# Stores of the expert gates moved from GpSimd's DMA queue to SyncE's, one at a time between weight loads

## The chip, the cores and the metric

The kernel runs on one core of a Trainium2 chip. The metric is the device time of one execution in microseconds. Before the change the median of three runs is 3434.36 us (3432.82 to 3434.39). The profile that is quoted below comes from one further execution, which took 3430.97 us; its span, from the first to the last instruction, is 3429.2 us. A difference of 0.2% is 6.9 us.

## The reference, cut to what matters

The model is one layer: an attention mixer, and then a mixture of 16384 experts (PEER), of which each token takes 16 for each of 8 heads. Only the second half matters here:

```
q = (xb @ w_q).reshape(PEER_BLOCK, PEER_HEADS, 2, PEER_HALF)
s = jnp.einsum('thcd,hcnd->thcn', q, sub_keys).astype(jnp.float32)
s1, i1 = lax.top_k(s[:, :, 0], PEER_TOPK)
s2, i2 = lax.top_k(s[:, :, 1], PEER_TOPK)
...
g = jax.nn.softmax(top_s, axis=-1).reshape(PEER_BLOCK, -1)
idx = idx.reshape(PEER_BLOCK, -1)
h = jnp.einsum('tkd,td->tk', u[idx], xb)
act = (g * jax.nn.gelu(h.astype(jnp.float32), approximate=False)).astype(xb.dtype)
return jnp.einsum('tk,tkd->td', act, v[idx])
```

Here `u` and `v` have 16384 rows of 2048 numbers each, and there are 512 tokens.

## The kernel before, in words

**Two ways to the experts.** The kernel treats 336 of the 512 tokens densely: it multiplies them with the whole of `u` and later with the whole of `v`, and sets to zero what the routing did not choose. The other 176 tokens go the sparse way: the chosen rows of `u` and `v` are gathered, 128 rows of 8 KB (1 MB) by one indirect DMA, and VectorE multiplies each such tile with the tokens (line 1619, 2.28 us each).

**The activations stage.** The change lies in the stage that multiplies with `u`, about 1450 to 2405 us of the profile. It runs over 128 pieces `e` of the key, each in two halves, so 256 halves. A half (`u_half`, line 1349) loads one weight block `wr` of 512 KB from `ut` by SyncE's DMA queue (line 264). ScalarE rounds it to `wh` (line 265), VectorE subtracts and leaves `wl` (line 266), and TensorE makes 8 times 3 products of 128x128 weights with 336 columns (lines 277 to 279). There are four buffers `wr` and about four pairs `wh` and `wl`, so the loads run some four halves ahead. After each pair of halves ScalarE takes the gelu into `hb` and sends it to DRAM, to `h_d` (168 KB, ScalarE's own DMA queue).

**Rows beside it.** The gathers (`row`, line 1605) are issued by GpSimd on its own DMA queue. Four row buffers are in turn, so GpSimd can issue a gather only when VectorE is done with an older row. Where a row product stands among VectorE's instructions is fixed when the program is built, and so VectorE waits in place for a row that has not landed, with the `wl` behind it.

**Gates beside it.** For the dense tokens the softmax weights must be spread over all 16384 experts. `gates_of` does this four tokens at a time in one PSUM bank (line 1504). `gate_out` copies banks with ScalarE into two buffers `gb`, one for each half of the experts (line 1528). Eight banks make a block of 32 tokens. When the last bank of a block is copied, four DMAs store the block to `g_d` in DRAM, two from each buffer (line 1535): 512 KB each, from 4 KB in a row per partition to runs of 512 B in DRAM (two 16-token groups of 4 experts, 4 bytes). Eleven blocks make 44 stores; the third block is half as large. The two buffers belong to the next block as soon as their stores have landed, so the first copy of the next block waits for them. `hold=3` says how many filled banks must be there before the first bank of a block is copied. The next stage reads `g_d` and `h_d`.

**What sets the order.** The program is written in one order and then scheduled: within an engine instructions keep a fixed order from then on, and an instruction waits in place. DMAs of SyncE go through hardware queue q1, those of ScalarE through q10, those of GpSimd through software queue q0. The 16 DMA engines serve all three.

Of the kernel before, what the change touches and what calls it, by code (L numbers as in the profile page):

```python
# [20 lines left out]
NOSYNC = mybir.DependencyInfo(mybir.DependencyClass.NoSync, mybir.DependencyReason.DATA)  # L21
# [30 lines left out]
SB = 16  # L52
# [3 lines left out]
NG = NK // GRP  # L56
# [178 lines left out]
def body(tc, nc, a, dbg=None):  # L235
    V, S, T, G, SP = nc.vector, nc.scalar, nc.tensor, nc.gpsimd, nc.sync
# [6 lines left out]
    def ps_tile(name="ps"):  # L243
        return pp.tile([P, 512], F32, name=name, tag="ps")

    more = {"n": 0, "pool": None, "of": (4, (1,)), "raw": None, "raws": 0}
# [8 lines left out]
    def wtile(src, eng=None, parts=False):  # L255
        more["n"] += 1
        extra = more["pool"] is not None and more["n"] % more["of"][0] in more["of"][1]
        w_ = more["pool"] if extra else wp
        raw = raw_half()
        hi = w_.tile([P, 1024], F32R, name="wh", tag="wh")  # L260
        lo = w_.tile([P, 1024], F32R, name="wl", tag="wl")

        def load(s):
            SP.dma_start(raw[:, s], src[:, s])
            more["last"] = S.activation(hi[:, s], raw[:, s], AF.Copy)  # L265
            more["lo"] = (eng or V).tensor_sub(lo[:, s], raw[:, s], hi[:, s].bitcast(F32))  # L266

        if parts:
            return hi, lo, load
        load(slice(0, 1024))  # L270
        return hi, lo

    def front(name, m=0, hf=0, eng=None, parts=False):
        return wtile(a["front"][FIDX[(name, m, hf)]], eng, parts)

    def mm3(ps, wh, wl, xh, xl, start, stop):
        T.matmul(ps, wl, xh, start=start, stop=False)  # L277
        T.matmul(ps, wh, xl, start=False, stop=False)  # L278
        T.matmul(ps, wh, xh, start=False, stop=stop)  # L279

    def split(hi, lo, src, eng=None):
        S.activation(hi, src, AF.Copy)
        (eng or V).tensor_sub(lo, src, hi.bitcast(F32))
# [30 lines left out]
    g_d = dp.tile([NG, P, ND // SB, GRP, SB], F32, name="g_d")  # L314
# [25 lines left out]
    xh = xq.tile([P, KC, XW], F32R, name="xh")[:, :, :LEN]  # L340
# [657 lines left out]
    def branch_tile(i):  # L998

        raw = raw_half()  # L1000
        SP.dma_start(raw, a["front"][FIDX[(*branch[i], 0)]])
        hi, lo = (wp.tile([P, D], F16, name=x, tag=x)[:, :1024] for x in ("wh", "wl"))
        scaled(hi, lo, raw, b_sc[:, i:i + 1])
        return hi, lo
# [133 lines left out]
    for m in range(KC):  # L1138
# [6 lines left out]
        wh, wl = branch_tile(m)  # L1145
        ps = ps_tile()
# [33 lines left out]
    with tc.tile_pool(name="outp", bufs=2, side="right") as op:  # L1180
# [13 lines left out]
        for m in range(KC):  # L1194
# [4 lines left out]
            wh, wl = wparts.pop(m)  # L1199
# [5 lines left out]
            ps = ps_tile()  # L1205
# [69 lines left out]
    def spread_rows():  # L1275
        b0 = ND - (NT - 1) * P
        SP.dma_start(eob_d, er[b0:])
        SP.dma_start(gwb_d, gw_all[b0:, NT - 1])
        for j, nt in enumerate(PARTS):
            t = slice(AT[j], AT[j + 1])  # L1280
            for to, of in ((eob, eob_d), (gwb, gwb_d)):
                SP.dma_start(to[:, t], of[t].rearrange("t (r k) -> (t r) k", k=nt))
# [65 lines left out]
    def u_half(ps, e, hf):  # L1348
        wh, wl = wtile(a["ut"][2 * e + hf])
        for kc in range(8):  # L1350
            s = slice(kc * P, (kc + 1) * P)
            kk = hf * 8 + kc
            mm3(ps[:, :ND], wh[:, s], wl[:, s], hgh[:, kk, :ND], hgl[:, kk, :ND], kk == 0, kk == KC - 1)

    early = route(3, 2, rk)
    with tc.tile_pool(name="score", bufs=2, side="left") as sp_, \
# [34 lines left out]
        for hc in range(16):  # L1391
            ps = ps_tile()
            for hf in range(2):
                wh, wl = wq.pop((hc, hf)) if (hc, hf) in wq else front("wq", hc, hf, G if hf and hc != 1 else V)
# [76 lines left out]
    def after_gelu(ins):  # L1471
        if "gelu" in more:
            tc.add_manual_dep(ins.ins, more["gelu"].ins.name, NOSYNC, reason="not before its block")
# [39 lines left out]
    banks = []  # L1513
    gs = {"sent": 0, "done": 0, "pool": None, "gated": False, "six": None}

    def gate_out(hold=3):

        for _ in range(min(2, len(banks))):
            if banks[0][1] % TB == 0 and len(banks) < hold:
                return  # L1520
            ps, tok, w = banks.pop(0)
            b, o = tok // TB, tok % TB
            wb = min(TB, ND - b * TB)
            if o == 0:
                gb["now"] = [vi.tile([P, D], F32, name="gb", tag="gin")[:, :NK // 2 * wb]
                             .rearrange("p (g b j t) -> p g b j t", b=wb // SB, j=GRP, t=SB) for _ in range(2)]
            for hf, half in enumerate(gb["now"]):
                after_gelu(S.activation(half[:, :, o // SB, :, o % SB:o % SB + w],
                                        ps.rearrange("p (t f g j) -> p f g j t", t=4, f=2, j=GRP)[:, hf, :, :, :w],
                                        AF.Copy, scale=1.0 / GW))  # L1530
                if o + w == wb:
                    for q in range(2):
                        g0 = hf * NG // 2 + q * NG // 4
                        b0 = b * TB // SB
                        G.dma_start(g_d[g0:g0 + NG // 4, :, b0:b0 + wb // SB].rearrange("g p b j t -> p g (b j t)"),
                                    half[:, q * NG // 4:(q + 1) * NG // 4].rearrange("p g b j t -> p g (b j t)"))

    routed = []

    def routing():  # L1540
        for ti in (2, 0, 1):
            yield from route(ti, 4, rk)
            routed.append(ti)
            while routed:
                yield

    def gating():
        for _ in range(NT):
            while not routed:
                yield  # L1550
            g_ = gates_of(routed[0])
            next(g_)
            routed.pop()
            yield
            yield from g_
        while banks:
            gate_out(1)
            yield
        gs["gated"] = True
# [3 lines left out]
    steps, gate_steps = routing(), gating()  # L1563
# [86 lines left out]
    def group_in(g):  # L1650

        if g in (0, 3):
            lent.clear()
        if not 0 < g < 3:
            lent["h"] = hin_tile()
            lent["g"] = vi.tile([P, D], F32, name="gin", tag="gin")[:, :GRP * ND].rearrange("p (b j t) -> p b j t", j=GRP, t=SB)
        held[g] = [lent["h"], lent["g"]]
        in_order(SP.dma_start(lent["h"], h_d[g]))
        in_order(SP.dma_start(lent["g"], g_d[g]))

    def gated(h, g):

        q = h.rearrange("p j (b t) -> p b j t", t=SB)
        in_order(V.tensor_mul(q, q, g))

    def rows_due(pos):
        while gs["done"] < np.interp(pos, PACE[0], PACE[1]):
            n = gs["done"]
            row_step(more["lo"], 6 if gs["six"] is not None and gs["six"] + 1 <= n < OWN - 6 else 4 if n < OWN - 4 else 3)
# [3 lines left out]
    for e in range(NK):  # L1673
        g = e // GRP
        if e == NK // 2:
            spread_rows()
        if e == NK - 4:
            assert next(steps, steps) is steps and next(gate_steps, steps) is steps
            assert gs["done"] >= OWN
            group_in(0)  # L1680
        ps = ps_tile() if e else ps0
        for hf in range(2):
            if (e, hf) != (0, 0):
                u_half(ps, e, hf)
            next(gate_steps, None)
            if (e, hf) == (NK - 1, 0):
                gated(*held[0])
                parts = {0: [vi.tile([P, D], F32R, name=x, tag=t)[:, :GRP * VW].rearrange("p (j t) -> p j t", t=VW)[:, :, :ND]
                             for x, t in (("vah", "gin"), ("val", "hin"))]}
                split(*parts[0], held.pop(0)[0])  # L1690
                group_in(1)
            if hf == 0:
                rows_due(e)
            for _ in range(1 if e < 20 or e % 2 else hf):
                next(steps, None)
        hb = up.tile([P, ND], F32, name="hb")
        more["gelu"] = S.activation(hb, ps[:, :ND], AF.Gelu)
        S.dma_start(h_d[g][:, e % GRP], hb)
        rows_due(e + 0.5)
# [102 lines left out]
    for i, step in enumerate(STEPS):  # L1802
        if i == NG - 1:
            assert gs["done"] == len(todo)
            ln_exp(more["last"])
            for j, y in enumerate((gw_all.rearrange("p a b -> p (a b)"), columns(2))):
                t = slice(ND + AT[j], ND + AT[j + 1])
                V.tensor_add(acc[:, :, t], acc[:, :, t], y.rearrange("p (c t) -> p c t", c=KC))
            for c in range(0, KC, 4):
                ps = ps_tile()  # L1810
# [7 lines left out]
        for qi, (g, q8) in enumerate(step):  # L1818
            wh, wl = wtile(a["vb"][at])
# [14 lines left out]
            for dc in range(2):  # L1834
# [7 lines left out]
                ps = banks_of.pop(c) if goes_on else ps_tile()  # L1842
# [44 lines left out]
```

## Time and profile before

| what | value |
|---|---|
| median of the runs | 3434.36 us |
| the profiled execution, its own time | 3430.97 us |
| its span | 3429.2 us |
| TensorE busy | 3393.8 us (99% of the span) |
| VectorE busy | 2627.0 us (77%) |
| ScalarE busy | 1707.2 us (50%) |
| mean rate of all DMAs | 272 GB/s |
| stores of full blocks of gates | 40, 512 KB each, 14.0 us from issue to landing (median) |
| weight loads of the stage | 256, 512 KB each, 8.6 us (median) |

In the profile a busy share is a mean over stages. TensorE is busy almost all the time, so what matters is where it waits, and what it then waits for. Lines are written as L277 for line 277. `PEclk` or the clock in a window is the share of full speed that TensorE was granted. A DMA queue's share is the time that its packets took, as a part of the time of 16 engines.

### The profile page before, as it was taken

Reading aid. Unit: us, or ns where it says so; the run is one execution under the profiler, and the core shown is the slowest. Engines: PE = TensorE matmul, PEld = TensorE weight load, DVE = VectorE, ACT = ScalarE, POOL = GpSimd, SP = SyncE. Lnnn points to the kernel's source line nnn. Section 1 sums busy time; section 2 is a strip of 40 time slices with the busy share of each in tenths; the row PEclk is TensorE's granted clock in tenths of the full one; section 3 lists DMA queues with packets and bytes.
Section 4 is the critical chain, followed back from the end, with each engine's and each line's share of the span. In section 5 each row is a group of like instructions: output and inputs, shape, how many; then the busy total and the mean of one; then the engine's idle time right before and its main releaser. Section 6 shows DMA issues by size and latency. Waiting matters only on the chain.

```text
span 3429.2 us, 54600 instructions
## 1 busy us (share of the span) xinstructions
PE 3393.8 (99%) x21188; PEld 2891.4 (84%) x21188; DVE 2627.0 (77%) x3829; ACT 1707.2 (50%) x2901; POOL 711.2 (21%) x526
## 2 busy tenths in 40 slices
PE   9999999999999999999999999999999999999998
PEld 8766666657764458899999999999999999999998
DVE  7744444446556668999989788887889899999996
ACT  6665665555465543334756666663433333333335
POOL 0000000000002221112222233334322222233330
PEclk9999999999999999999999999999999999999999
DMA  6443443333256442379999999999999999999993
GB/s 235 136 145 131 140 133 111 133 111 105 80 180 214 154 137 91 102 278 355 353 382 348 381 415 414 411 416 414 385 373 377 385 389 385 393 401 396 402 386 113
DMA packets 236372, 933.39 MB, mean 272 GB/s; under 512 B 27120, under 2 KB 52688, under 8 KB 190928
## 3 DMA queue, kind: packets, MB, share of 16 engines
q1 hardware_dynamic: 142672, 487.40, 39.2%
q0 software_dynamic: 58160, 396.32, 29.0%
q10 hardware_dynamic: 35280, 46.18, 3.8%
q8 instruction: 166, 2.72, 0.3%
q14 instruction: 94, 0.77, 0.1%
HBM read 861.59 MB, written 68.21 MB: 271 GB/s over the span
## 4 chain that ended last, share of the span: by engine, by line
PE 81%; DVE 5%; issue 5%; DMA 5%; POOL 2%; ACT 1%; SPq 0%; POOLq 0%; DVEq 0%; ACTq 0%
PE ps L277 26%; PE ps L278 25%; PE ps L279 25%; DMA row<-u,eo 2%; POOL row L1605 1%; DVE wl L266 1%; DMA wr<-ut 1%; DMA row<-u,eob 1%; PE ps L1504 1%; DVE xgb L1623 1%; DVE row L1619 1%; DMA wr<-vb 0%; DMA hin<-h_d 0%; ACT wh L265 0%; PE ps L965 0%
## 5 line engine op out<-in xcount | busy, mean ns | idle before, releaser
L265 ACT ACTIVATE wh<-wr 128x1024 fp32r<-128x1024 f32 (+1 forms) x578 | 604.6, 1053 | 914.3 <-PE ps L279 648.3
L266 DVE TENSOR_TENSOR wl<-wr,wh 128x1024 fp32r<-128x1024 f32 (+1 forms) x565 | 680.7, 1215 | 150.2 <-ACT wh L265 147.9
L277 PE MATMUL ps<-hgh,wl 128*128 128x336 f32 (+1 forms) x2304 | 755.3, 328 | 10.0 <-DVE wl L266 10.0
L278 PE MATMUL ps<-hgl,wh 128*128 128x336 f32 (+1 forms) x2304 | 746.6, 324 | 0.0
L279 PE MATMUL ps<-hgh,wh 128*128 128x336 f32 (+1 forms) x2304 | 745.9, 324 | 0.0
L277 PE MATMUL ps<-vah,wl 128*128 128x336 f32 x2048 | 645.6, 315 | 2.4 <-DVE wl L266 2.4
L279 PE MATMUL ps<-vah,wh 128*128 128x336 f32 x2048 | 645.2, 315 | 0.0
L278 PE MATMUL ps<-val,wh 128*128 128x336 f32 x2048 | 645.2, 315 | 0.0
L277 PEld LDWEIGHTS ps<-hgh,wl 128*128 128x128 f32 x2304 | 433.1, 188 | 21.9 <-DVE wl L266 12.3
L279 PEld LDWEIGHTS ps<-hgh,wh 128*128 128x128 f32 x2304 | 433.1, 188 | 10.3 <-issue 0.2
L278 PEld LDWEIGHTS ps<-hgl,wh 128*128 128x128 f32 x2304 | 433.5, 188 | 9.6 <-issue 0.2
L277 PE MATMUL ps<-xnh,wl 128*128 128x512 f16 (+1 forms) x1184 | 392.7, 332 | 0.0
L279 PE MATMUL ps<-xnh,wh 128*128 128x512 f16 (+1 forms) x1184 | 392.6, 332 | 0.0
L278 PE MATMUL ps<-xnl,wh 128*128 128x512 f16 (+1 forms) x1184 | 392.6, 332 | 0.0
L277 PEld LDWEIGHTS ps<-vah,wl 128*128 128x128 f32 x2048 | 384.4, 188 | 2.7 <-DVE wl L266 2.7
L278 PEld LDWEIGHTS ps<-val,wh 128*128 128x128 f32 x2048 | 384.4, 188 | 0.0
L279 PEld LDWEIGHTS ps<-vah,wh 128*128 128x128 f32 x2048 | 384.4, 188 | 0.0
L1619 DVE SCALAR_TENSOR_TENSOR row<-row,xg 128x2048 f32<-128x2048 f32 x128 | 292.3, 2284 | 20.9 <-DMA row<-u,eo 20.8
L279 PEld LDWEIGHTS <-wh 128*128 128x128 f16 x1696 | 165.9, 98 | 143.9
L277 PEld LDWEIGHTS <-wl 128*128 128x128 f16 x1696 | 168.8, 100 | 135.2 <-issue 1.8
L278 PEld LDWEIGHTS <-wh 128*128 128x128 f16 x1696 | 165.9, 98 | 131.8 <-issue 0.3
L1605 POOL DMA_INDIRECT row<-u,eo x128 | 164.8, 1287 | 520.8 <-DVE row L1619 441.4
(608 smaller groups left out, 5378.9 us busy)
## 6 DMA issues: line engine op xcount, KB each, us to landing
wr<-ut SPq DMA_DIRECT2D x256, 512.0 KB, 8.6
wr<-vb SPq DMA_DIRECT2D x256, 512.0 KB, 7.8
wr<-front SPq DMA_DIRECT2D x164, 512.0 KB, 4.0
xr<-front SPq DMA_DIRECT2D x58, 512.0 KB, 4.6
h_d<-hb ACTq DMA_DIRECT2D x128, 168.0 KB, 8.1
gin<-g_d SPq DMA_DIRECT2D x32, 672.0 KB, 11.5
hin<-h_d SPq DMA_DIRECT2D x32, 672.0 KB, 8.9
g_d<-gb POOLq DMA_DIRECT2D x40, 512.0 KB, 14.0
```

The source lines that it names most:

```text
L265: more["last"] = S.activation(hi[:, s], raw[:, s], AF.Copy)
L266: more["lo"] = (eng or V).tensor_sub(lo[:, s], raw[:, s], hi[:, s].bitcast(F32))
L277: T.matmul(ps, wl, xh, start=start, stop=False)
L278: T.matmul(ps, wh, xl, start=False, stop=False)
L279: T.matmul(ps, wh, xh, start=False, stop=stop)
L1504: T.matmul(bank[:, o:o + P], ohs[q % 4][:, 1, :, t], wos[:, q % 3, c, :, t], start=c == 1, stop=c == 0)
L1605: G.indirect_dma_start(out=row, out_offset=None, in_=a[src], in_offset=bass.IndirectOffsetOnAxis(ap=idx, axis=0))
L1619: ins = V.scalar_tensor_tensor(row, row, 1.0, x, ALU.mult, ALU.mult, accum_out=wk)
L1623: ins = V.scalar_tensor_tensor(x, row, wk, x, ALU.mult, ALU.add)
```

## The change

Three things are changed. The stores of a block are no longer issued by GpSimd when the block is full: they are put in a list, `to_store`. In each half of the stage, after its products, one of them is taken from the list and issued by SyncE, in the queue of the weight loads; a dependency without a wait keeps it from being scheduled ahead of that half's last product. And `hold` goes from 3 to 4, so that the first copy of a block is written when four banks are there.

```diff
@@ def mm3
-        T.matmul(ps, wh, xh, start=False, stop=stop)
+        more["pe"] = T.matmul(ps, wh, xh, start=False, stop=stop)
@@
-    def gate_out(hold=3):
+    def gate_out(hold=4):
...
-                        G.dma_start(g_d[g0:g0 + NG // 4, :, b0:b0 + wb // SB].rearrange("g p b j t -> p g (b j t)"),
-                                    half[:, q * NG // 4:(q + 1) * NG // 4].rearrange("p g b j t -> p g (b j t)"))
+                        to_store.append((g_d[g0:g0 + NG // 4, :, b0:b0 + wb // SB].rearrange("g p b j t -> p g (b j t)"),
+                                         half[:, q * NG // 4:(q + 1) * NG // 4].rearrange("p g b j t -> p g (b j t)")))
+
+    to_store = []
+
+    def store_gates():
+
+        if to_store:
+            ins = SP.dma_start(*to_store.pop(0))
+            tc.add_manual_dep(ins.ins, more["pe"].ins.name, NOSYNC, reason="not before its place")
...
             if (e, hf) != (0, 0):
                 u_half(ps, e, hf)
+            store_gates()
             next(gate_steps, None)
```

TensorE's instructions keep their order. On SyncE the four stores of a block now stand between weight loads. This is SyncE after the change, at the eighth block (its buffers are gb_20848 and gb_20849):

```order
L264 DMA wr_21546<-ut 128x1024
L1543 DMA g_d_78<-gb_20848 128x8x128
L264 DMA wr_21591<-ut 128x1024
L1543 DMA g_d_78<-gb_20848 128x8x128
L264 DMA wr_21642<-ut 128x1024
L1543 DMA g_d_78<-gb_20849 128x8x128
L264 DMA wr_21686<-ut 128x1024
L1543 DMA g_d_78<-gb_20849 128x8x128
L264 DMA wr_21733<-ut 128x1024
```

Before, nothing but weight loads stood here, and the four stores stood on GpSimd, between two gathers. This is GpSimd before, where the ninth block's stores stand (gb_21487 and gb_21488):

```order
L1605 DMA row_22045<-u,eob_11479 128x2048
L1605 DMA row_22093<-u,eob_11479 128x2048
L1535 DMA g_d_78<-gb_21487 128x8x128 x2
L1535 DMA g_d_78<-gb_21488 128x8x128 x2
L1605 DMA row_22134<-u,eob_11479 128x2048
L1605 DMA row_22182<-u,eob_11479 128x2048
```

After the change these gathers follow each other without a store between them. The third place is ScalarE, where the ninth block's first bank is copied. Before (gb_21487 and gb_21488 are the ninth block's buffers, and wh the rounded weights):

```order
L265 ACTIVATE wh_21458<-wr_21457 128x1024
L1698 DMA h_d_77<-hb_21314 128x336
L265 ACTIVATE wh_21506<-wr_21505 128x1024
L1510 ACTIVATE wos_13513<-rh__10118,wt_13515 128x128 x4
L1510 ACTIVATE wos_13513<-more_oh_13512,wt_13515 128x128 x4
L1697 ACTIVATE hb_21403<-ps_21320 128x336
L1528 ACTIVATE gb_21487<-ps_21265 128x16x4x4
L1698 DMA h_d_77<-hb_21403 128x336
L1528 ACTIVATE gb_21488<-ps_21265 128x16x4x4
```

The same place after the change (the ninth block's buffers are now gb_21576 and gb_21577):

```order
L265 ACTIVATE wh_21547<-wr_21546 128x1024
L1707 DMA h_d_77<-hb_21403 128x336
L265 ACTIVATE wh_21592<-wr_21591 128x1024
L1510 ACTIVATE wos_13513<-rh__10118,wt_13515 128x128 x4
L1510 ACTIVATE wos_13513<-more_oh_13512,wt_13515 128x128 x4
L1706 ACTIVATE hb_21492<-ps_21409 128x336
L1528 ACTIVATE gb_21576<-ps_21262 128x16x4x4
L1707 DMA h_d_77<-hb_21492 128x336
L1528 ACTIVATE gb_21577<-ps_21262 128x16x4x4
L265 ACTIVATE wh_21643<-wr_21642 128x1024
L265 ACTIVATE wh_21687<-wr_21686 128x1024
```

The first copy of the block now stands two roundings of weights later. In SyncE's rows above, the last store of gb_20849, for which the copy into gb_21577 waits, stands behind the load of wr_21686. Its rounding, and that of wr_21642, come on ScalarE only after this copy.

More of the change, by code (lines that the diff above doesn't have):

```diff
@@ L1677, in body @@
         if e == NK - 4:
-            assert next(steps, steps) is steps and next(gate_steps, steps) is steps
+            assert next(steps, steps) is steps and next(gate_steps, steps) is steps and not to_store
             assert gs["done"] >= OWN
```

## Prediction

> **What bounds the kernel now.** I read the page first: TensorE is busy almost all the time.
>
> ```profile
> span 3429.2 us, 54600 instructions
> ...
> PE 3393.8 (99%) x21188; PEld 2891.4 (84%) x21188; DVE 2627.0 (77%) x3829; ACT 1707.2 (50%) x2901; POOL 711.2 (21%) x526
> ```
>
> So a change that leaves TensorE's work alone can win only what TensorE waits, 35.4 us in the whole span, or add to it. Where in the activations stage does it wait? The windows (instructions' busy time in each stretch, then clock, DMA share and GB/s) tell it by place.
>
> ```profile
> 1860.00:1940.00 80.00, 80.00 (x573) 78.72 (x573) 69.06 (x77) 53.21 (x130) 27.86 (x23) 1.00 0.97 367
> 1940.00:2340.00 400.00, 398.38 (x2804) 392.46 (x2803) 340.34 (x371) 256.29 (x614) 136.17 (x111) 1.00 1.02 414
> 2340.00:2360.00 20.00, 16.71 (x103) 16.44 (x102) 11.24 (x9) 6.07 (x7) 8.69 (x5) 0.95 1.02 411
> 2360.00:2380.00 20.00, 20.00 (x128) 20.00 (x128) 18.17 (x18) 5.49 (x7) 15.94 (x7) 0.97 1.02 417
> ```
>
> Two things are to be seen. From 1940 us on the DMA engines are full (share 1.02, 414 GB/s), and before that they are not. And TensorE loses 1.62 us in 400 us, then 3.29 us in one place, after which its clock is granted at 0.95 and 0.97. TensorE's own waits, for 2040 to 2365 us and for 2365 to 2420 us:
>
> ```profile
> PE ps L277 <- DVE wl L266: 4.9, 3, 3.3
> ...
> PE ps L277 <- DVE wl L266: 2.7, 2, 1.5
> ```
>
> The longest of the first three is followed back in the timeline of GpSimd and VectorE.
>
> ```profile
> 2328.20 0.94 POOL L1605 DMA_INDIRECT row<-u,eob  x1 [4.85 <-DVE row L1619]
> 2329.13 3.65 POOL L1535 DMA_DIRECT2D g_d<-gb  x4
> 2333.08 1.41 POOL L1605 DMA_INDIRECT row<-u,eob  x1 [0.30 <-issue]
> ...
> 2343.38 1.22 DVE L266 TENSOR_TENSOR wl<-wr,wh 128x1024 fp32r<-128x1024 f32 x1
> 2353.33 2.29 DVE L1619 SCALAR_TENSOR_TENSOR row<-row,xgb 128x2048 f32<-128x2048 f32 x1 [8.73 <-DMA row<-u,eob]
> 2355.55 2.35 DVE L266 TENSOR_TENSOR wl<-wr,wh 128x1024 fp32r<-128x1024 f32 x2
> ```
>
> Four stores of gates stand in GpSimd's queue ahead of a gather. The gather, issued at 2333.1, lands at 2353; VectorE waits 8.73 us for it, and two `wl` are stuck behind. TensorE waits 3.3 of these 8.73 us, so it had about 5.4 us of weights in hand. That is the lead on which the rest turns. All waits of this kind, of 1940 to 2365 us:
>
> ```profile
> ACT wh L265 <- DMA wr<-ut: 71.9, 39, 2.9
> ...
> DVE row L1619 <- DMA row<-u,eo: 20.0, 4, 7.7
> ...
> DVE row L1619 <- DMA row<-u,eob: 14.9, 3, 8.7
> ACT gb L1528 <- DMA g_d<-gb: 12.0, 4, 5.1
> ```
>
> VectorE waits 34.9 us for rows in seven waits, ScalarE 12.0 us in four for stores. ScalarE waits 39 times for a weight load: most loads land just when they are needed.
>
> **The change part by part.** First what goes.
>
> ```profile
> L1535 POOL DMA_DIRECT2D g_d<-gb x44: 887/928/992, 1673.0 to 2331.9; - x44
> ...
> L264 SPq DMA_DIRECT2D wr<-ut x256: 327/328/403, 1416.9 to 2430.8; - x128
> ```
>
> GpSimd loses 44 issues of 0.93 us, SyncE gains 44 of some 0.33 us, as for its loads; neither is near its limit, and this is worth nothing by itself. The gathers no longer stand behind the stores, so I take off the row waits' part of TensorE's time: 4.9 us, and the clock's loss after the longest, 0.05 x 20 + 0.03 x 20 = 1.6 us. That is 6.5 us. The 2.7 us after 2365 us lie behind the last store and stay; what if they went too is a bound below.
>
> Then what comes. The stores are the same bytes, in the queue of the weights. The queues in the full stretch, 1940 to 2340 us (packets, MB, share of 16 engines; below, issues and median us to landing):
>
> ```profile
> q0 software_dynamic: 15871, 103.93, 63.0%
> q1 hardware_dynamic: 14444, 52.62, 32.7%
> q10 hardware_dynamic: 7200, 8.60, 5.9%
> ...
> wr<-ut SPq DMA_DIRECT2D x100, 512.0 KB, 10.0
> g_d<-gb POOLq DMA_DIRECT2D x24, 512.0 KB, 14.6
> ...
> row<-u,eo POOLq DMA_INDIRECT x48, 11.3
> ```
>
> There are six bursts of four stores here, 12.6 MB. Weights take q1 at 131 GB/s (100 loads of 0.524 MB in 400 us, one in 4 us). And between bursts, 2098 to 2134 us:
>
> ```profile
> q0 software_dynamic: 1252, 9.11, 60.7%
> q1 hardware_dynamic: 1366, 5.01, 34.2%
> ...
> wr<-ut SPq DMA_DIRECT2D x10, 512.0 KB, 12.7
> ```
>
> With rows queued, q1 gets 5.01 MB in 36 us, 139 GB/s: hardly more than the weights need. A store ahead of a load in q1 then costs that load 0.524 MB / 139 GB/s = 3.8 us, four cost 15.1 us. This is the upper bound: 15.1 - 5.4 of lead = 9.7 us of waiting per burst. Lower bound: with no rows queued q1 gets all 414 GB/s, four stores take 5.1 us, the lead covers them, and TensorE waits 0. Which of the two? With the stores gone from it q0 needs 91.3 of the 165.6 MB that 414 GB/s move in 400 us, q10 8.6; 65.7 MB are left for q1, which now wants 65.2. So the engines are full to the last, and q1 gets 164 GB/s on the mean. Four stores at that rate take 12.8 us; in the four halves over which they go out, 16 us, the 33 GB/s that weights leave carry 0.53 MB, 3.2 us; 9.6 us of lateness against 5.4 us of lead leave 4.2 us. While VectorE waits for weights it frees no row buffers, gathers stop, and q1 gets their share, 63%; so I take somewhat over half of the 4.2 us, 2.4 us per burst. Six bursts are 14.4 us. Before 1940 us I take nothing: the DMAs are not full there, and the lead covers the stores.
>
> ScalarE is the second place. In the order printed above, the copy into the ninth block's second buffer waits for a store that stands behind two weight loads, both of which ScalarE rounds only after this copy. Queued behind it are those two `wh`, then their `wl`, then TensorE. Where the next copy comes two halves later than before, it moves by some 8 us, and the store's landing moves by its place behind two more loads and three stores. Today's longest such wait is 5.1 us. I keep it inside the 2.4 us, as the store and the loads share one queue, but it pushes towards the upper bound. The one bank more that stays filled costs TensorE nothing as long as the eight PSUM banks come round: none of TensorE's waits above is for ScalarE. If that cover went, the price would be one such copy's wait, up to 5.1 us per burst.
>
> The sum against the profiled execution: 3430.97 - 6.5 + 14.4 = 3438.9 us. The median of the runs is 3.4 us above that execution, so the forecast is 3442.3 us, 7.9 us slower.
>
> **The rivals.** *Heavy: the hardware queue moves the stores in short packets.* A store's runs in DRAM are 512 B. How queues cut runs is seen from 1268 to 1287 us, where GpSimd loads runs of 1344 B (xn) and ScalarE stores 64 KB in rows of 512 B (xc_d), and in the burst at 2145 to 2150 us (last row, q0 with stores):
>
> ```profile
> q0 software_dynamic: 768, 2.75, 46.2%
> ...
> q10 hardware_dynamic: 144, 0.07, 1.9%
> ...
> xn<-ht_d POOLq DMA_DIRECT2D x15, 168.0 KB, 4.1
> xc_d<-sc ACTq DMA_DIRECT2D x1, 64.0 KB
> ```
>
> ```profile
> q0 software_dynamic: 326, 1.21, 63.1%
> ```
>
> q0 has 3.6 KB per packet where the runs are 1344 B, and 3.7 KB with the stores: it joins runs. q10 has one packet per run. Its 64 KB took 1.9% of 19 us on 16 engines, 5.8 us; eight times that is 46 us of engine time for 512 KB, 2.9 us on all 16. On q0 a store takes 0.524/1.21 x 63.1% x 5 us = 1.4 us. With 1.5 us more for each of 24 stores, in a stretch where the engines are full, TensorE loses 36 us: 3434.4 - 6.5 + 36 = 3463.9 us. It decides if the packets on q1 are much smaller than 4 KB. Against it: the source of a store is 4 KB in a row, which no hardware DMA of this trace with short runs has, so the cut may follow the source. [...]
>
> *Even: nothing is won or lost.* The same bytes go through the same full engines; rows came late before, weights come late now, and TensorE's lead covers either alike: 3434 us, within 4. For it: the balance above, 65.7 against 65.2 MB. It decides if VectorE's waiting gives back nearly all. [...]
>
> *Gain: all three waits go.* Rows come in time, and stores one by one are covered by the lead: 3434.4 - 6.5 = 3427.9 us, and 3425.2 us if the later 2.7 us went too. For it: each store leaves the queue a half to recover. Against it: q1 has no room while rows are queued. It decides if q0 is idle more than the 1.02 lets one think.
>
> **How the numbers follow.** Forecast 0.45, heavy 0.17, even 0.27, gain 0.11. The forecast alone spans 3434 us (1.1 us per burst) to 3453 us (4.2 us per burst). 0.2%, 6.9 us, is about what a measurement of this kernel can tell from no change; its upper edge, 3441.2 us, lies within the forecast, of which I count 0.27 above and 0.18 below. Slower is 0.27 + 0.17 = 0.44, the same 0.18 + 0.27 = 0.45, faster 0.11. The range goes from 3428 us, which leaves out most of the gain, to 3462 us, which leaves out half of the heavy case: about 0.19 outside.
>
> **What would show it.** In the changed profile VectorE's waits for rows between 1940 and 2365 us should nearly vanish from 34.9 us, and the rows land sooner than in 11.3 us. ScalarE's waits for `wr` should grow past 71.9 us, with weight loads behind a store landing after 15 us and more, and TensorE's waits for `wl` should stand after each burst from the sixth on, 2 to 4 us each. If q1's packets are near 0.5 KB in a burst, the heavy case is there. If TensorE's waits from 2040 to 2365 us are under 3 us in all, I am wrong, and the loads did not suffer.

## The result, and the profile after

The changed kernel takes 3478.06 us (median, 3474.53 to 3481.08) and the kernel before 3434.16 us. The ratio is 1.0133, with a 95% interval of 1.0121 to 1.0145: 43.9 us slower. The forecast was 7.9 us slower; its heavy rival, with another mechanism, 29.5.

The page's head for the changed kernel (its profiled execution took 3474.53 us) shows what kind of time was added.

```profile
span 3472.7 us, 54597 instructions
...
PE 3407.6 (98%) x21188; PEld 2901.7 (84%) x21188; DVE 2627.5 (76%) x3829; ACT 1709.6 (49%) x2901; POOL 663.4 (19%) x482
```

The span grew by 43.5 us. TensorE's idle time went from 35.4 to 65.1 us, 29.7 more. Its busy time, for the same 21188 matmuls, grew by 13.8 us. So a third of the loss is not waiting but slower matmuls. The windows of the changed kernel (columns as before: PE, PEld, DVE, ACT, POOL, granted clock, DMA share, GB/s), first the full stretch, then three pieces of it:

```profile
1940.00:2340.00 400.00, 374.52 (x2573) 367.24 (x2573) 314.96 (x344) 236.35 (x565) 102.34 (x81) 0.96 0.99 386
...
2020.00:2060.00 40.00, 33.34 (x220) 32.35 (x220) 26.62 (x31) 22.53 (x57) 9.19 (x8) 0.91 0.91 341
...
2180.00:2220.00 40.00, 37.67 (x268) 36.84 (x268) 26.33 (x30) 21.87 (x55) 9.54 (x7) 1.00 0.90 337
...
2260.00:2300.00 40.00, 32.91 (x212) 32.22 (x210) 28.96 (x33) 24.23 (x61) 9.68 (x8) 0.87 0.89 337
```

The full stretch held 398.38 us of TensorE's work before and holds 374.52 now, at a clock of 0.96 where it was 1.00. The share of the DMA engines hardly fell, 0.99 where it was 1.02, but they move 386 GB/s where it was 414. By this row alone it can't be told whether the engines or the order in a queue makes the loads late; the sixth and the ninth experiment below tell it.

What TensorE waits for from 1940 to 2400 us, in the changed kernel:

```profile
PE ps L1504 <- ACT wos L1510: 19.9, 12, 6.9
PE ps L277 <- DVE wl L266: 5.5, 2, 5.1
```

The forecast looked for waits of L277 for `wl`. Most of the waiting now is L1504, the gate products, for ScalarE's `wos`; before, that wait was not there at all. The other engines' waits, of 1940 to 2365 us:

```profile
DVE wl L266 <- ACT wh L265: 88.5, 33, 11.0
ACT wh L265 <- DMA wr<-ut: 75.1, 26, 12.6
ACT gb L1528 <- DMA g_d<-gb: 26.9, 7, 8.1
```

VectorE's waits for rows, 34.9 us before, no longer stand in this list. ScalarE's waits for weights went from 71.9 to 75.1 us, the longest from 2.9 to 12.6. Its copies' waits for stores went from 12.0 us in four to 26.9 in seven. One burst shows how these meet. SyncE and ScalarE of the changed kernel, from 2238 us:

```profile
2238.23 0.43 SPq L1543 DMA_DIRECT2D g_d<-gb  x1
2241.93 0.33 SPq L264 DMA_DIRECT2D wr<-ut  x1
2242.30 5.83 SPq L1543 DMA_DIRECT2D g_d<-gb  x1
2248.22 4.70 SPq L264 DMA_DIRECT2D wr<-ut  x1
2252.97 1.57 SPq L1543 DMA_DIRECT2D g_d<-gb  x1
2254.64 4.97 SPq L264 DMA_DIRECT2D wr<-ut  x1
2259.66 1.01 SPq L1543 DMA_DIRECT2D g_d<-gb  x1
```

```profile
2256.58 1.06 ACT L265 ACTIVATE wh<-wr 128x1024 fp32r<-128x1024 f32 x1 [7.08 <-DMA wr<-ut]
2257.55 1.30 ACT L1510 ACTIVATE wos<-more_oh,wt 128x128 f16<-128x128 f16 x4
...
2261.84 0.39 ACT L1528 ACTIVATE gb<-ps 128x256 f32<-128x256 f32 x1 [1.52 <-DMA g_d<-gb]
...
2270.24 0.94 ACT L1528 ACTIVATE gb<-ps 128x256 f32<-128x256 f32 x3 [8.02 <-DMA g_d<-gb]
2271.05 2.01 ACT L265 ACTIVATE wh<-wr 128x1024 fp32r<-128x1024 f32 x2
2272.94 1.31 ACT L1510 ACTIVATE wos<-rh__10118,wt 128x128 f16<-128x128 f16 x4
```

And TensorE at this place, behind the rows of its waits in two other bursts:

```profile
2050.04 0.65 PE L277 MATMUL ps<-hgh,wl 128*128 128x336 f32 x1 [5.10 <-DVE wl L266]
...
2202.20 0.28 PE L1504 MATMUL ps<-wos,rh__10118 128*128 128x128 f16 x2 [2.03 <-ACT wos L1510]
...
2273.73 0.37 PE L1504 MATMUL ps<-wos,rh__10118 128*128 128x128 f16 x2 [6.88 <-ACT wos L1510]
```

First ScalarE waits 7.08 us for the weight load issued at 2241.93, which stands behind the first store. Then it waits 8.02 us for the last store of the block, issued at 2259.66, before it may copy into the same buffer at 2270. Queued behind this copy are two `wh` and four `wos`. The two `wh` then run back to back, so their loads had come meanwhile. TensorE uses up its lead and waits 6.88 us at the gate product. The mean clock of that piece is 0.87. In the pieces above it is below 1.00 where a single wait was 5.10 or 6.88 us, and 1.00 where the longest was 2.03 us.

One more thing is new in SyncE's rows: issues that took 0.33 us now take up to 5.83 us.

### The profile page after: what moved, and what is told of

Read it like the earlier page. It is cut to its first block, busy times and chain, and to the rows that moved or that the text cites. A ratio compares the mean times of both kernels' runs of the same rounds, so it can differ in the third digit from the quotient of the medians.

```text
span 3472.7 us, 54597 instructions
## 1 busy us (share of the span) xinstructions
PE 3407.6 (98%) x21188; PEld 2901.7 (84%) x21188; DVE 2627.5 (76%) x3829; ACT 1709.6 (49%) x2901; POOL 663.4 (19%) x482
## 3 DMA queue, kind: packets, MB, share of 16 engines
q1 hardware_dynamic: 188432, 509.42, 40.5%
## 4 chain that ended last, share of the span: by engine, by line
PE 58%; issue 17%; DMA 8%; DVE 7%; POOL 6%; ACT 2%; SPq 0%; POOLq 0%; DVEq 0%; ACTq 0%
PE ps L277 18%; PE ps L278 18%; PE ps L279 18%; POOL row L1613 5%; DMA wr<-ut 3%; DVE row L1627 2%; DVE wl L266 2%; DMA g_d<-gb 2%; POOL lists L1613 1%; ACT wh L265 1%; PE ps L1504 1%; ACT wos L1510 1%; DMA row<-u,eo 0%; DVE xg L1631 0%; DMA hin<-h_d 0%
## 5 line engine op out<-in xcount | busy, mean ns | idle before, releaser
L277 PE MATMUL ps<-hgh,wl 128*128 128x336 f32 (+1 forms) x2304 | 760.7, 330 | 17.3 <-DVE wl L266 17.3
L277 PE MATMUL ps<-vah,wl 128*128 128x336 f32 x2048 | 645.7, 315 | 2.5 <-DVE wl L266 2.5
L277 PEld LDWEIGHTS ps<-hgh,wl 128*128 128x128 f32 x2304 | 437.1, 190 | 30.3 <-DVE wl L266 20.6
L277 PE MATMUL ps<-xnh,wl 128*128 128x512 f16 (+1 forms) x1184 | 392.7, 332 | 0.0
L277 PEld LDWEIGHTS ps<-vah,wl 128*128 128x128 f32 x2048 | 384.7, 188 | 2.7 <-DVE wl L266 2.7
L277 PEld LDWEIGHTS <-wl 128*128 128x128 f16 x1696 | 168.7, 99 | 135.4 <-issue 1.8
```

## The experiments

All times are medians, compared with runs of the kernel before on the same chip (3432.91, 3431.51, 3432.18 and 3432.81 us in the four groups). What a kernel is over before is the difference to its own group; differences between two kernels of these are uncertain by some 5 to 8 us, as their intervals tell. "Copies" are ScalarE's copies into gb, L1528.

**First: stores that no copy waits for.** The stores read the activations hgh in place of gb, so what is stored is not the gates.

```diff
-    half[:, q * NG // 4:(q + 1) * NG // 4].rearrange("p g b j t -> p g (b j t)")))
+    hgh.bitcast(F32).rearrange("p k s -> p (k s)")[:, :m_].rearrange("p (g r) -> p g r", g=NG // 4)))
```

> The stores go out at the same places from SyncE, in the same 512-B pieces, but they read the activations, which nothing rewrites here, and not gb; so no copy has to wait for a store (the gates in DRAM are then not the gates). Theory 'copy': the 44 us come from ScalarE's copy, which waits for a store's landing (47.1 us in ten waits) and holds up the wos and wh queued behind it; then nearly all comes back: 3433 to 3442 us, and TensorE's waits at the gate products (19.9 us from 1940 to 2400 us) fall under 3 us. Theory 'queue' (the prediction's: weight loads land late behind the stores in SyncE's queue): the loads are as late as before, and it stays at 3465 us or more, with TensorE's waits for wl as long as now or longer.

3448.21 us, ratio 1.0044 (1.0028 to 1.0061): 15.3 us over before. That is in neither theory's range: 28.6 of the 43.9 us went, 15.3 stayed. Waits from 1540 to 2460 us of this kernel:

```profile
ACT wh L265 <- DMA wr<-ut: 142.5, 58, 13.7
...
PE ps L1504 <- ACT wos L1510: 13.0, 6, 7.4
...
PE ps L277 <- DVE wl L266: 6.9, 5, 2.8
```

No copy waits for a store any more, but the weights are as late as in the changed kernel (147.1 us, 12.6 at most; before, 117.1 and 7.3), and it is again mostly `wos` that TensorE waits for: on ScalarE they stand behind the `wh` whose load is late. So there are two causes, the copies with about 29 us and something in the weights' queue with 15.

One more wait of ScalarE hangs on the stores, and the list of waits has it under another name. ScalarE of this kernel:

```profile
2018.91 1.31 ACT L1510 ACTIVATE wos<-more_oh,wt 128x128 f16<-128x128 f16 x4
2024.99 0.33 ACTq L1708 DMA_DIRECT2D h_d<-hb  x1
2025.42 1.32 ACT L1510 ACTIVATE wos<-rh__10118,wt 128x128 f16<-128x128 f16 x4 [5.20 <-DMA g_d<-hgh]
```

No `wos` needs a store. ScalarE stands at its own issue of `h_d` until a DMA of SyncE's has landed, mostly a store of gates. The changed kernel's trace shows it at one place: a store issued at 2014.68 us reports on semaphore 109, whose last update for it comes at 2028.03, and the issue of `h_d` at 2028.10, 0.07 us later, reports on 109 too. All 1027 DMAs of SyncE and all 245 of ScalarE there report on the same eight semaphores. Such waits of over 0.5 us are 30.8 us in four issues here and 21.4 us in six in the changed kernel, where four end with a store and two with a weight load; before there were none. What they cost by themselves was not tested. In the two longest here, 12.4 and 12.1 us, the next weight load landed over 1 us later still, and the sixth experiment has only 5.5 us of them at nearly the same price.

**Second: the same, but 4 KB in a row in DRAM.** Stores of gb on SyncE; g_d is written as a flat array, so the gates lie there in another order and the output isn't the reference's.

```diff
-    to_store.append((g_d[g0:g0 + NG // 4, :, b0:b0 + wb // SB].rearrange("g p b j t -> p g (b j t)"),
+    to_store.append((flat[o_:o_ + P * m_].rearrange("(p r) -> p r", p=P),
```

> The stores stay on SyncE, at the same places, with the copies as they are; only the order of the floats in DRAM is changed, so that each partition writes 4 KB in a row and not eight runs of 512 B (the gates lie in another order in DRAM). Theory 'packets': a store of 1024 pieces of 512 B takes turns with rows of 8 KB and so needs 3 to 15 us from its first to its last piece; with 128 pieces of 4 KB the four stores and the loads between them land in some 17 us where it was 24, the copy's wait falls from 47.1 to about 15 us, and the time comes to 3434 to 3446 us. Theory 'place' (whatever stands behind or ahead of weight loads in one queue lands late, the pieces do not matter): 3470 us or more.

3463.54 us, ratio 1.0093 (1.0076 to 1.0110): 30.6 us over before, 13.3 less than the changed kernel. Again between the two. Of the mechanism, one half was wrong: the copies still wait 47.5 us.

```profile
ACT wh L265 <- DMA wr<-ut: 119.8, 50, 6.8
...
ACT gb L1528 <- DMA g_d<-gb: 47.5, 9, 11.7
```

What short pieces made worse is the loads: the longest wait for one is 6.8 us here and 12.6 with 512-B pieces.

**Third: the same stores, singly, from GpSimd.**

```diff
-    ins = SP.dma_start(*to_store.pop(0))
+    ins = G.dma_start(*to_store.pop(0))
```

> The changed kernel with the stores on GpSimd's queue: singly, at the same places, next block's copies one bank later. If SyncE's queue (its pieces and its loads) is what costs the 44 us: 3428 to 3437 us, copy waits under 15 us, the row waits of 34.9 us about halved, as a gather stands behind one store and not four. If going out singly, later, is what costs: the last store of a block still goes out 16 us later than in a burst, the copies wait over 30 us, and it stays above 3455 us.

3442.53 us, ratio 1.0027 (1.0018 to 1.0037): 9.6 us over before, between the ranges. Most of the loss is SyncE's queue. But the second expectation was right about the copies, which wait as long as in the changed kernel:

```profile
ACT gb L1528 <- DMA g_d<-gb: 47.9, 10, 10.3
```

So it is the spacing that makes them wait: the last store of a block goes out 8.4 to 14.5 us after the first here and 16.2 to 27.1 us in the changed kernel, where it was 2.7 to 2.9 us before.

**Fourth: only the copies later, in the kernel before.**

```diff
-    def gate_out(hold=3):
+    def gate_out(hold=4):
```

> The kernel before with only the last part of the change: next block's copies one bank later, the stores in bursts of four on GpSimd. If that part is harmless: ScalarE's copy wait falls from 14.8 to under 5 us, TensorE's 35.4 us of waits stay, 3431 to 3436 us. If the bank that stays filled longer costs TensorE: waits of TensorE for gb's copy appear, 3440 us or more.

3434.85 us, ratio 1.0005 (0.9996 to 1.0015). As the harmless case said: no copy waits for a store, and TensorE waits for neither a bank nor ScalarE. This part of the change costs nothing that can be measured.

**Fifth: the changed kernel, copies one bank later still.**

```diff
-    def gate_out(hold=4):
+    def gate_out(hold=5):
```

> The changed kernel with next block's copies two banks later than before instead of one. Where the first experiment freed the copies by giving the stores another source, here they still wait for their stores, but come two halves (about 8 us) later. Theory 'copy': the ten waits of 47.1 us, the longest 10.1, shrink to under 10 us in all, and the time comes near the first experiment's 3448: 3444 to 3454 us. Theory 'bank': a bank that stays filled still longer holds up TensorE's gate products; then waits of TensorE for the gb copy or for banks appear, and it stays over 3460 us.

3452.57 us, ratio 1.0059 (1.0043 to 1.0074), 21.1 us over before: "copy" was right. TensorE's waits from 1940 to 2400 us and the copies' waits of this kernel:

```profile
PE ps L1504 <- ACT wos L1510: 18.3, 8, 7.5
...
ACT gb L1528 <- DMA g_d<-gb: 2.4, 2, 1.9
```

With the computation whole, 22.8 us come back as the copies' waits fall from 47.1 to 2.4 us. What stays is the first experiment's rest, within the intervals.

**Sixth: the first and the second together.** What is stored is not the gates.

```diff
-    half[:, q * NG // 4:(q + 1) * NG // 4].rearrange("p g b j t -> p (g b j t)")))
+    hgh.bitcast(F32).rearrange("p k s -> p (k s)")[:, :m_]))
```

> The first and the second experiment together: stores on SyncE that no copy waits for, and with 4 KB in a row in DRAM (what is stored is not the gates). What the first one left, 15 us, is then put to the test: if it is weight loads that land late because 512-B pieces take turns with 8-KB rows, it shrinks to 2 to 8 us (3435 to 3441 us). If it is the mere place of 0.52 MB ahead of a load in one queue, it stays: 3444 to 3450 us.

3444.91 us, ratio 1.0042 (1.0027 to 1.0057), 13.4 us over before: the place in the queue costs nearly all of the rest. From the first experiment's 15.3 us it can't be told apart. With copies that don't wait, short pieces are worth little.

**Seventh: four stores at once on SyncE.**

```diff
-    if to_store:
+    while to_store:
```

> The changed kernel with a block's four stores all at once on SyncE, at the first of the four places. Theory 'queue': the next load now stands behind four stores, some 17 us, so weights come later than singly: wl and wh waits grow, 3470 us or more. Theory 'copy': the last store goes out some 16 us sooner, so the copies wait less than half of 47.1 us, and it falls to 3450 to 3462 us.

3485.22 us, ratio 1.0163 (1.0148 to 1.0179), 53.7 us over before. "Queue" was right: the copies themselves no longer wait, but the loads are later than ever. ScalarE also stands 26.9 us, at seven issues of `h_d`, until a store or a load has landed.

```profile
ACT wh L265 <- DMA wr<-ut: 164.9, 44, 15.8
...
PE ps L1504 <- ACT wos L1510: 34.1, 17, 7.3
```

So on SyncE going out singly is the better of the two, by 9.8 us, little more than the uncertainty; on GpSimd, with copies one bank later, bursts are (3434.9 against 3442.5 us, the fourth and the third).

**Eighth: singly on GpSimd, copies two banks later than before.** The third's edit and the fifth's.

```diff
-    def gate_out(hold=4):
+    def gate_out(hold=5):
...
-    ins = SP.dma_start(*to_store.pop(0))
+    ins = G.dma_start(*to_store.pop(0))
```

> The stores singly on GpSimd's queue, with next block's copies two banks later than before. The third experiment's 3442.5 us held 47.9 us of copy waits; 'copy' says that they fall under 10 us and the time to 3428 to 3435 us, at or just below the kernel before, since row waits (28 us against 34.9) and the bursts both go. If singly is bad by itself, or a bank longer costs TensorE: 3439 us or more.

3434.12 us, ratio 1.0007 (0.9998 to 1.0016): as "copy" said, the same as before. Copies wait 5.6 us. But nothing is gained. VectorE still waits 39.2 us for rows, as with bursts (34.9 us before); that single stores ahead of the gathers cause it, as bursts did, is likely but not shown:

```profile
DVE row L1627 <- DMA row<-u,eo: 24.0, 8, 7.3
DVE row L1627 <- DMA row<-u,eob: 15.2, 8, 4.5
```

**Ninth: the sixth's stores from ScalarE.** What is stored is not the gates.

```diff
-    ins = SP.dma_start(*to_store.pop(0))
+    ins = S.dma_start(*to_store.pop(0))
```

> As the sixth (no copy waits for a store, 4 KB in a row; what is stored is not the gates), but ScalarE issues the stores, so that they stand in its queue beside the small stores of the products and not among the weight loads. The sixth took 3444.9 us. Theory 'queue': the 12 us or so that are left there are weight loads standing behind stores; then they go: 3429 to 3437 us. Rival 'sharing': a hardware queue of any engine takes its turn against rows and loads, and the loads are late either way: 3441 us or more.

3432.01 us, ratio 0.9998 (0.9989 to 1.0008). "Queue" was right: with the same stores at the same places, in another hardware queue than the loads, the 13.4 us are gone. Its queues from 1940 to 2340 us:

```profile
q0 software_dynamic: 12466, 90.73, 54.8%
q1 hardware_dynamic: 14428, 52.55, 32.8%
q10 hardware_dynamic: 10609, 20.92, 13.5%
```

The stores (24, 12.6 MB) are in q10, and the loads keep pace: 52.55 MB, as before (52.62). In all, the DMA engines moved 412 GB/s in this stretch, and 404 in the sixth; which loads were late was decided by the queue that the stores stood in, and that was worth 13 us here.

**Tenth: no stores at all.** The later load of gates reads the products h_d, so the output isn't the reference's.

```diff
-    ins = SP.dma_start(*to_store.pop(0))
-    tc.add_manual_dep(ins.ins, more["pe"].ins.name, NOSYNC, reason="not before its place")
+    to_store.pop(0)
...
-    in_order(SP.dma_start(lent["g"], g_d[g]))
+    in_order(SP.dma_start(lent["g"].rearrange("p b j t -> p (b j t)"), h_d[g].rearrange("p j n -> p (j n)")))
```

> The changed kernel without any store of gates (the later load of gates reads the products instead, so the output isn't the reference's); copies and their order as changed. It shows what the stores cost at all and what the later copies cost without them. If the prediction's first term holds (6.5 us of TensorE's time were due to gathers behind stores) and the later copies are harmless: 3424 to 3430 us, with row waits under 5 us. If the one bank later costs TensorE, or TensorE's waits are not due to the stores: 3432 us or more.

3421.48 us, ratio 0.9970 (0.9959 to 0.9982): 10.7 us under before, more than either range allowed. No placing of the same stores can be expected to win more. TensorE has no wait at all from 1940 to 2400 us. The interval, 6 to 14 us, holds the 6.5 us that the prediction took off.

**Eleventh: ScalarE issues the stores of gb, in 512-B pieces; copies two banks later than before.** The ninth's edit and the fifth's, on the changed kernel.

```diff
-    def gate_out(hold=4):
+    def gate_out(hold=5):
...
-    ins = SP.dma_start(*to_store.pop(0))
+    ins = S.dma_start(*to_store.pop(0))
```

> The stores singly from ScalarE, of gb and in 512-B pieces as in the changed kernel, copies two banks later than before (nothing left out). The ninth showed a queue free of weight loads with 4-KB pieces at 3432.0 us. Left open is what the short pieces do to the engine that issues them: with them SyncE's own issues were held, 231 us for 256 loads where they take 84. If ScalarE is held as SyncE is, by 1 to 3 us per store, its wh and wos come late and it takes 3440 us or more. If the holding came from the row of loads in that queue alone: 3430 to 3437 us.

3471.21 us, ratio 1.0111 (1.0096 to 1.0127), 38.4 us over before. ScalarE is held in the act of issuing: such waits ahead of `wos` are 69.1 us in twelve. Its rows in one burst:

```profile
2176.35 5.21 ACTq L1707 DMA_DIRECT2D h_d<-hb  x1
2181.59 3.18 ACTq L1543 DMA_DIRECT2D g_d<-gb  x1
2184.87 0.44 ACT L1510 ACTIVATE wos<-rh__10118,wt 128x128 f16<-128x128 f16 x1 [7.60 <-issue]
```

The holding follows the 512-B pieces and not the loads: here, in a queue without the loads, issues of `h_d` took up to 14.0 us; among stores of 4 KB the loads took 0.79 us at most to issue in the second and 1.99 us in the sixth, and in the ninth ScalarE's stores of 4 KB took 0.70 us at most.

**Twelfth: the eighth, copies three banks later than before.**

```diff
-    def gate_out(hold=4):
+    def gate_out(hold=6):
...
-    ins = SP.dma_start(*to_store.pop(0))
+    ins = G.dma_start(*to_store.pop(0))
```

> The best of the forms with the full computation taken one step further: stores singly on GpSimd, copies three banks later than before. The eighth (two banks later) took 3434.1 us with 5.6 us of copy waits left. If the copies are the last thing that costs: under 1 us of copy waits and 3429 to 3434 us, the same as the kernel before within what can be measured. If the banks that stay filled now hold up TensorE: waits of ScalarE's or TensorE's for banks and 3437 us or more.

3432.11 us, ratio 0.9999 (0.9990 to 1.0008). The copies' waits are gone, and it is the kernel before within what can be measured. None of these kernels with the whole computation beats it.

## Why the prediction was wrong, and where it was right

The direction was right, and so was the queue as one cause. Where the size failed:

**The step that failed: "I keep it inside the 2.4 us, as the store and the loads share one queue."** That was ScalarE's copy. It was worth 28.6 us (the changed kernel less the first experiment), or 22.8 by the fifth; either is well over the 14.4 us that the bursts were to cost in all. Three things were wrong in that step. The copy's wait was bounded by the longest of before, 5.1 us; singly, behind loads, the longest was 10.1 us, and there were ten waits, 47.1 us in all. Behind the copy I counted `wh` and `wl`, but not the `wos`, for which TensorE's gate products wait. And "none of TensorE's waits above is for ScalarE" was taken as cover, though it only said that ScalarE had not been late before. The price without that cover, up to 5.1 us per burst, was named, but it went into no sum and got no chance. The rise of the waits is no measure of the price: 47 to 48 us of copy waits cost 22.8 to 28.6 us on SyncE with short pieces, 17.2 with 4 KB in a row (the second less the sixth) and 7.0 on GpSimd (the third's 9.6 less the eighth's 2.6, whose copies are freed by place and not by source). That the lead is what differs was only argued: the later the loads already are, the less lead a copy's wait finds.

**The bursts' price, 14.4 us, was the right mechanism and too small.** The first experiment is 15.3 us over before; with the 6.5 us that went, the bursts cost 21.8 us, 3.6 each instead of 2.4. The 4.2 us that the prediction had before it took off what stopped gathers give back was nearer. The sixth and the ninth show that it is indeed the place in the weights' queue. The forecast's own range, 3434 to 3453 us, holds the first experiment's 3448.2. Where it shows was wrong: TensorE waits for `wos` more than for `wl`, since both `wh` and `wos` come from ScalarE in order.

**The clock was counted on one side only.** I took 1.6 us off for the drop that went, and added nothing for the waits that came. TensorE's busy time grew by 13.8 us in all.

**"Neither is near its limit, and this is worth nothing by itself," of the issues.** SyncE's issues were priced at 0.33 us. The rows for the stores and the loads of the changed kernel (ns, least, median, most) say otherwise:

```profile
L1543 SPq DMA_DIRECT2D g_d<-gb x44: 383/1016/8682, 1678.1 to 2396.3; - x44
...
L264 SPq DMA_DIRECT2D wr<-ut x256: 327/328/10417, 1417.0 to 2474.4; - x128
```

Summed over the trace's records, the 256 loads took 231 us to issue where they took 84. With 4 KB in a row they take 85. What this holding alone costs on SyncE is not settled: with copies that don't wait it is within the 1.9 us between the first and the sixth, and with copies that wait it is somewhere in the 13.3 us that 4 KB gave back.

**Before 1940 us "I take nothing": wrong for the copies, right for the queue.** Of 400 us from 1540 on, TensorE worked all 400 before, 392.47 in the changed kernel and 398.76 in the first experiment.

**Right:** the row waits nearly vanish; the copies one bank later cost TensorE nothing by themselves (the fourth; the twelfth, with three banks). The 6.5 us that the row waits cost lie within the tenth experiment's interval, at its lower end.

**The heavy rival** came nearest in time, and its premise holds: q1 on the page went from 142672 to 188432 packets. Its price does not: the changed kernel's trace has 27 ns for a 512-B packet of q1 (the median), so by estimate 1024 of them, spread over 16 engines, are 1.7 us, 0.3 more than the 1.4 us that the prediction had for a store on q0, and not 1.5 more. Where copies don't wait, short pieces against long ones made 1.9 us (the first less the sixth), so that its time came nearest is luck.

## What to carry to other kernels

Before a DMA is moved to another queue, list what waits for its landing in a buffer that is used again, and everything that stands in order behind that waiter on its engine, down to the engine that bounds the kernel; waits of 7 and 8 us on an engine that is busy half the time cost nearly 7 us on the one that is busy 99% of it. Stores put among loads that land just when they are needed made them late and cost 13.4 us (the sixth), while the same stores in a queue without those loads cost nothing that can be measured (the ninth, ratio 0.9998), with the DMA engines as busy (a share of 1.00 in the sixth and 1.02 in the ninth, from 1940 to 2340 us). A count of zero waits is no cover: ask how much lead there is, and whether two delays draw on the same lead.

## What the runs showed of the hardware

**Short pieces in a hardware queue held the engine that issued them.** Eight runs of 512 B per partition, 1024 in a store, made about 1040 packets on q1 for each store of the changed kernel. The issues next to such stores took up to 14.4 us on SyncE (a weight load of the first experiment) and 14.0 us on ScalarE (a store of products of the eleventh), so other DMAs of that engine were held too. With 4 KB in a row the stores' issues took at most 1.6 us on SyncE (the second). GpSimd's queue joined the runs in the kernel before, with about 138 packets on q0 for each store, and its stores took 0.99 us at most to issue.

**How long such a store took depended on what shared the engines.** Two pieces of the changed kernel's DMA, in each of which q1 moves about one store and one load: from 2314.1 to 2329.0 us, with rows on q0, and from 2334.9 to 2337.7 us, without.

```profile
q0 software_dynamic: 681, 4.99, 79.5%
q1 hardware_dynamic: 1107, 1.02, 19.5%
```

```profile
q1 hardware_dynamic: 1121, 0.97, 102.8%
```

About as many packets of q1 passed in 14.9 us beside rows as in 2.8 us without them: 68 GB/s against 346. The first 9.9 us of the first piece, to 2324 us, show the two queues side by side:

```profile
q0 software_dynamic: 478, 3.51, 84.0%
q1 hardware_dynamic: 476, 0.45, 13.0%
```

The two queues passed nearly as many packets, 478 against 476, but 3.51 MB against 0.45. Of q0's packets 428 were of 8 KB; of q1's 401 were of 512 B and 60 of 4 KB; the rest, on both, were of 4 B. So in these 9.9 us the queue of mostly 512-B packets got as many packets as the one of 8-KB packets beside it, and an eighth of its bytes.
